# Feed-forward input matrix by seven products of quarter sums instead of eight of quarters, two of the four weight sums made by adding DMAs

## The chip, the cores and the metric

The kernel runs on one core of a Trainium2 chip. TensorE (PE) multiplies, VectorE (DVE) and ScalarE (ACT) do the elementwise work, GpSimd (POOL) does a little elementwise work, SyncE (SP) issues DMAs. The metric is device time in microseconds of one execution, the median of several runs. Smaller is better.

## The reference, cut to what matters

One layer of a streaming encoder on 544 tokens (512 of a prompt, 32 of a sample), model width 1024: attention, a recurrent branch and cross-attention are merged into `x`, and a feed-forward part of width 2816 follows. Only this last part is touched:

```
h2 = rms_norm(x, lp["norm_ffn"])                        # 544 x 1024
g_ff, u_ff = jnp.split(h2 @ lp["w_ffn_in"], 2, axis=-1) # w_ffn_in 1024 x 5632, two halves of 2816
x = x + (jax.nn.silu(g_ff) * u_ff) @ lp["w_ffn_out"]    # w_ffn_out 2816 x 1024
```

Everything is float32. To reach that accuracy at the speed of one pass, each operand is split into a high part `h` (rounded to the format fp32r) and a low part `l` (the remainder), and a product is taken as `wh*xh + wh*xl + wl*xh`: three matmuls for one.

## The kernel before

Activations lie transposed: 128 channels on the partitions, 544 tokens along the row, eight such tiles for 1024 channels (k = 0 to 7). A weight chunk is 1024 x 256, 1 MB, loaded by one DMA from SP into a `raw` buffer (there are two). It gives two weight tiles (j = 0, 1) of 128 output channels: ACT rounds 128x1024 elements into `wh` (function `A`, line 236), DVE subtracts to get `wl` (function `LO`, line 249). There are three `wh` and three `wl` buffers.

`gemm` makes one output tile of 128 channels x 544 tokens in `acc`, a pair of PSUM banks of 272 tokens each: 8 k x 3 products x 2 halves = 48 matmuls of 272 columns. All matmuls are recorded under line 308. There are two `acc` buffers.

Feed-forward: `ffn_in(i)` runs over pairs of a gate chunk and an up chunk. For each gate tile `ff_gate` multiplies by the row norm `rb` (DVE) and takes silu (ACT); for each up tile `ff_up` multiplies by `rb` and by the gate (DVE), and rounds and subtracts the result into `fh`, `flo` (tiles `ah`, `al` or `bh`, `bl`). `ffn_out(i)` multiplies by `w_ffn_out` and adds to `x2`. The 22 hidden tiles go in three parts of 8, 8 and 6: in 0, in 1, out 0, in 2, out 1, out 2. The norm factor `rb` does not exist when the first feed-forward matmul starts: the matmuls run on `x * norm_ffn` (`xgh`, `xgl`), and `rb` is applied at the evacuation. Just ahead of the feed-forward part lies the output projection `w_out`, whose evacuation (`out_evac`) makes `x2`, `xgh`, `xgl`, the squares and, after the eighth tile, `rb`.

The program's order on each engine is fixed when it is built. A planner (`Flow`) keeps a clock of estimated costs, and each piece of work is written out when its inputs are due in that plan; on the chip every engine then takes its list in order and waits for semaphores. So a late input on one engine holds up all that is listed behind it there.

Of the kernel before, what the change touches and what calls it, by code (L numbers as in the profile page):

```python
# [9 lines left out]
F32 = mybir.dt.float32  # L10
# [37 lines left out]
class Flow:  # L48
# [141 lines left out]
def hybrid_step(ctx: ExitStack, tc, io):  # L190
# [18 lines left out]
    def tl(pool, shape, dt, tag, bufs=1):  # L209
        return pool.tile(shape, dt, name=tag, tag=tag, bufs=bufs)  # L210
# [93 lines left out]
            fl.ready(out, t + 2200)  # L304
        return t + 2200

    def MM(out, lhsT, rhs, start, stop):
        nc.tensor.matmul(out, lhsT=lhsT, rhs=rhs, start=start, stop=stop)  # L308
# [41 lines left out]
    FF_PARTS = [(0, 8), (8, 8), (16, 6)]  # L350
    c_fi, c_fo = [None] * 3, [None] * 3
    for kind, i in (("in", 0), ("in", 1), ("out", 0), ("in", 2), ("out", 1), ("out", 2)):
        f0, nf = FF_PARTS[i]
        if kind == "in":
            c_fi[i] = [[chunk("w_ffn_in", 11 * s + f0 // 2 + c) for s in (0, 1)] for c in range(nf // 2)]
        else:
            c_fo[i] = [chunk("w_ffn_out", c, f0, nf) for c in range(4)]

    NQ = 2
    raws = {}  # L360
# [2 lines left out]
    def load_weights():  # L363
        for i, (src, nk) in enumerate(chunks):
            yield from fl.take("raw")
            raw = slot_tile(wpool, [P, 8, 256], F32, "raw")
            raws[i] = raw
            t = 0.0
            for j in range(2) if i == 0 else (None,):
                if j == 1:  # L370
                    yield from fl.get("mem dma")
                cs = slice(0, 256) if j is None else slice(j * P, (j + 1) * P)
                t = dma(raw[:, :nk, cs], src[:, :, cs], nk * P * (1024 if j is None else 512))
                if j is not None:
                    fl.set(("raw", i, j), t)
                    fl.set(("raw", i, j, "sent"))
            fl.set(("sent", i))
            for j in range(2):
                if ("raw", i, j) not in fl.ev:
                    fl.set(("raw", i, j), t)  # L380

    def split_weights():
        for i, (src, nk) in enumerate(chunks):
            if i in c_mem[4:]:
# [12 lines left out]
                fl.give("raw", t2)  # L397
                continue
            for j in range(2):
                yield from fl.get(("raw", i, j))  # L400
                yield from fl.take("wh", "wl")
                wh = slot_tile(wpool, [P, 8, P], F32R, "wh")[:, :nk]
                wl = slot_tile(wpool, [P, 8, P], F32R, "wl")[:, :nk]
                r = raws[i][:, :nk, j * P:(j + 1) * P]
                t = VC(wh, r) if fl.free["V"] + 1500 < fl.free["A"] else A(wh, r)
                wts[i, j] = (wh, wl)
# [4 lines left out]
            fl.give("raw", t2)  # L411

    def gemm(tiles, xh, xl, n=T, need=None):

# [3 lines left out]
        def products(acc, c, j, seq, first, last):  # L418
            wh, wl = wts[c, j]
            for q, (a, b, k) in enumerate(seq):  # L420
                w, x = (wl if a else wh), (xl if b else xh)
                for hf, m in halves:
                    s = slice(hf * m, (hf + 1) * m)
                    MM(acc[:, hf, :m], w[:, k, :], x[k][:, s] if isinstance(x, list) else x[:, k, s],
                       start=first and q == 0, stop=last and q == len(seq) - 1)
                yield None

        def finish(acc, c, j, evac):
            fl.give("wh")
# [1094 lines left out]
        return go  # L1524


    acts = [None] * 3

    def ff_gate(i, n):
        def go(acc):  # L1530
# [25 lines left out]
            fl.set(("f", i, n), t)  # L1556
        return go

    def ffn_in(i):
        f0, nf = FF_PARTS[i]  # L1560
        pool, a, b = (actp, "ah", "al") if i % 2 == 0 else (S["actb"], "bh", "bl")
        acts[i] = (tl(pool, [P, KD, T], F32R, a), tl(pool, [P, KD, T], F32R, b))
        for c in range(nf // 2):
            need = (lambda k: ("xg", k)) if i == 0 and c == 0 else None
            yield from gemm([(c_fi[i][c][0], j, ff_gate(i, 2 * c + j)) for j in range(2)], xgh, xgl, need=need)
            yield from gemm([(c_fi[i][c][1], j, ff_up(i, 2 * c + j)) for j in range(2)], xgh, xgl)

    def fo_evac(fp, i, n):
        def go(acc):
            t = VT(b2(x2[:, n]), acc[:, :, :HT], b2(x2[:, n]), OP.add)  # L1570
            give_acc(t)
            if i < 2:
                return
            yield t
            yield from square_sum(S["sq"][0], n)
        return go
# [42 lines left out]
    def ffn_out(fp, i):  # L1619
        f0, nf = FF_PARTS[i]  # L1620
        fh, flo = acts[i]
        split = 0 if i < 2 else LAST
        tiles = [(c_fo[i][n // 2], n % 2, n) for n in range(KD)]
        for n0 in range(0, KD - split, 2):
            yield from gemm([(c, j, fo_evac(fp, i, n)) for c, j, n in tiles[n0:min(n0 + 2, KD - split)]], fh, flo,
                            need=None if n0 else (lambda k: ("f", i, k)))
        if not split:
            return

        for t0, m_ in ((0, 256), (256, T - 256)):  # L1630
            for c, j, n in tiles[KD - split:]:
                yield from fl.get(("wh", c, j))
                yield from fl.take("acc")
                acc = slot_tile(accp, [P, 2, 512], F32, "acc")[:, 0, :m_]
                for q, (a, k) in enumerate([(a, k) for a in range(2) for k in range(nf)]):
                    if a == 1 and k == 0:
                        yield from fl.get(("wl", c, j))
                    for x in (fh, flo) if a == 0 else (fh,):
                        MM(acc, wts[c, j][a][:, k], x[:, k, t0:t0 + m_], q == 0 and x is fh,
                           q == 2 * nf - 1)  # L1640
                    yield None
                fl.spawn(last_evac(fp, n, (t0, m_), acc), fl.now + 60)
# [5 lines left out]
    def main():  # L1648
# [77 lines left out]
        xgh = tl(hpool, [P, KD, T], F32R, "hh")  # L1726
        xgl = tl(hpool, [P, KD, T], F32R, "hl")
# [12 lines left out]

# [4 lines left out]
def host_arrays(inputs):  # L1745
# [21 lines left out]
        a[n] = i[n].reshape(1, 64)  # L1767
    for n in ("w_in", "w_mem_kv", "w_proj_a", "w_proj_b", "w_proj_c", "w_gate", "w_out", "w_ffn_in", "w_ffn_out"):
        a[n] = tiles(i[n][0])
    rel = np.arange(REL_LO, REL_LO + REL_N)  # L1770
    n = np.abs(rel)
    large = 8 + sum((n >= t).astype(np.int64) for t in (12, 16, 23, 32, 46, 64, 91))
# [44 lines left out]
```

## Time and profile before

| | |
|---|---|
| median of 3 runs | 1230.53 us (1229.99 to 1231.04) |
| the profiled execution | 1230.78 us |
| its span, first to last instruction | 1229.0 us |
| PE busy | 1214.2 us, 99% |
| DVE busy | 678.9 us, 55% |
| ACT busy | 466.0 us, 38% |
| POOL busy | 28.2 us, 2% |
| feed-forward part | 814.2 us to the end |

The profile is of one execution. Busy time of PE is modelled, since matmuls are pipelined: the distance between the starts of two matmuls says what one costs, not its duration. On DVE and ACT too the duration of an instruction is some 0.08 us longer than the distance to the next one where two follow each other without a wait.

### The profile page before, as it was taken

How to read it: one execution, taken by the hardware profiler on the slowest of the kernel's cores; microseconds unless marked ns; L12 is line 12 of the kernel's file. 1: busy time of each engine (PE TensorE's matmuls, PEld its weight loads, DVE VectorE, ACT ScalarE, POOL GpSimd, SP SyncE). 2: the span in 40 equal slices, each digit the busy share in tenths (PEclk: the TensorE clock that was granted, in tenths of full speed). 3: DMA queues.
4: the chain of work that ended last, by engine and by line, in shares of the span. 5: the costliest groups of instructions: out<-in, count | busy, mean ns of one | idle time of the engine just before them, and what ended most of it. 6: DMA issues, size and time to landing. Idle time of an engine off the chain costs nothing.

```text
span 1229.0 us, 22475 instructions
## 1 busy us (share of the span) xinstructions
PE 1214.2 (99%) x9620; PEld 1205.5 (98%) x9620; DVE 678.9 (55%) x1340; ACT 466.0 (38%) x781; POOL 28.2 (2%) x88
## 2 busy tenths in 40 slices
PE   8999999999999999999999999999999999999996
PEld 8999999999999999999999999999999999999996
DVE  6886878787257777654455244544443443344335
ACT  6635454444335665532333232332222221222122
POOL 0002000000001001000000000000000000000001
PEclk8999999999999999999999999999999999999998
DMA  7772343321222223323422413131323222222212
GB/s 261 233 272 96 133 138 116 106 87 54 103 97 94 78 73 109 122 69 121 140 95 76 176 69 104 69 104 69 103 70 103 72 101 90 82 96 77 87 52 73
DMA packets 36835, 131.19 MB, mean 107 GB/s; under 512 B 4184, under 2 KB 15832, under 8 KB 25088
## 3 DMA queue, kind: packets, MB, share of 16 engines
q1 hardware_dynamic: 36736, 129.76, 30.9%
q8 instruction: 75, 1.23, 0.4%
q14 instruction: 24, 0.20, 0.0%
HBM read 118.81 MB, written 13.68 MB: 108 GB/s over the span
## 4 chain that ended last, share of the span: by engine, by line
PE 96%; DVE 2%; DMA 1%; ACT 0%; issue 0%; SPq 0%; DVEq 0%; ACTq 0%
PE acc L308 86%; PE side L308 8%; PE side L315 2%; DMA mk_d<-mkf 1%; DMA raw<-in_w_mem_kv 0%; DVE x L258 0%; DVE wl L249 0%; DVE xT L258 0%; DVE rst L249 0%; DVE al L249 0%; ACT wh L236 0%; DVE m L249 0%; ACT m L236 0%; SPq L300 0%; DVE hl L249 0%
## 5 line engine op out<-in xcount | busy, mean ns | idle before, releaser
L308 PE MATMUL acc<-hh,wh 128*128 128x272 f32 x1856 | 387.1, 289 | 0.0
L308 PE MATMUL acc<-hl,wh 128*128 128x272 f32 x1856 | 385.8, 289 | 0.0
L236 ACT ACTIVATE wh<-raw 128x1024 fp32r<-128x1024 f32 (+1 forms) x179 | 187.4, 1048 | 351.2 <-PE acc L308 328.3
L308 PEld LDWEIGHTS acc<-hh,wh 128*128 128x128 f32 x1856 | 290.7, 189 | 0.3
L308 PEld LDWEIGHTS acc<-hl,wh 128*128 128x128 f32 x1856 | 290.0, 188 | 0.1
L249 DVE TENSOR_TENSOR wl<-raw,wh 128x1024 fp32r<-128x1024 f32 (+1 forms) x180 | 217.1, 1207 | 95.6 <-PE acc L308 73.6
L308 PE MATMUL acc<-hh,wl 128*128 128x272 f32 x1856 | 257.2, 288 | 0.0
L308 PEld LDWEIGHTS acc<-hh,wl 128*128 128x128 f32 x1856 | 241.5, 188 | 0.1
L249 DVE TENSOR_TENSOR t<-acc,rb 128x544 f32<-128x544 f32 x44 | 31.9, 725 | 150.3 <-PE acc L308 150.0
L308 PE MATMUL acc<-ah,wh 128*128 128x272 f32 (+2 forms) x480 | 101.4, 288 | 0.0
L308 PE MATMUL acc<-al,wh 128*128 128x272 f32 (+2 forms) x480 | 101.4, 289 | 0.0
L249 DVE TENSOR_TENSOR x<-acc,x 128x544 f32<-128x544 f32 (+2 forms) x35 | 23.6, 675 | 102.7 <-PE acc L308 102.7
L308 PE MATMUL acc<-bl,wh 128*128 128x272 f32 x384 | 79.7, 289 | 0.0
L308 PE MATMUL acc<-bh,wh 128*128 128x272 f32 x384 | 79.6, 288 | 0.0
L308 PEld LDWEIGHTS acc<-ah,wh 128*128 128x128 f32 x480 | 76.4, 188 | 0.0
L308 PEld LDWEIGHTS acc<-al,wh 128*128 128x128 f32 x480 | 76.2, 188 | 0.0
L308 PE MATMUL acc<-ah,wl 128*128 128x272 f32 (+2 forms) x480 | 66.0, 288 | 0.0
L308 PEld LDWEIGHTS acc<-ah,wl 128*128 128x128 f32 x480 | 62.4, 188 | 0.0
L308 PEld LDWEIGHTS acc<-bh,wh 128*128 128x128 f32 x384 | 60.1, 189 | 0.0
L308 PEld LDWEIGHTS acc<-bl,wh 128*128 128x128 f32 x384 | 60.0, 188 | 0.0
L308 PE MATMUL acc<-bh,wl 128*128 128x272 f32 x384 | 54.0, 289 | 0.0
L308 PEld LDWEIGHTS acc<-bh,wl 128*128 128x128 f32 x384 | 50.0, 188 | 0.0
(250 smaller groups left out, 1318.1 us busy)
## 6 DMA issues: line engine op xcount, KB each, us to landing
raw<-in_w_in SPq DMA_DIRECT2D x24, 1024.0 KB, 4.9
raw<-in_w_ffn_in SPq DMA_DIRECT2D x22, 1024.0 KB, 4.9
raw<-in_w_gate SPq DMA_DIRECT2D x12, 1024.0 KB, 4.9
raw<-in_w_ffn_out SPq DMA_DIRECT2D x8, 1024.0 KB, 4.9
raw<-in_w_mem_kv SPq DMA_DIRECT2D x7, 1024.0 KB, 6.1
raw<-in_w_proj_a SPq DMA_DIRECT2D x4, 1024.0 KB, 4.9
raw<-in_w_proj_b SPq DMA_DIRECT2D x4, 1024.0 KB, 4.8
raw<-in_w_proj_c SPq DMA_DIRECT2D x4, 1024.0 KB, 4.9
```

The costliest lines, as they stand in the source:

```text
L236: nc.scalar.activation(out, in_, func, scale=scale, bias=bias, accum_out=accum_out)
L249: nc.vector.tensor_tensor(out, a, b, o)
L308: nc.tensor.matmul(out, lhsT=lhsT, rhs=rhs, start=start, stop=stop)
L315: nc.tensor.transpose(out, in_, ident[:n, :n])
```

## The change

`w_ffn_in` is handled as 22 chunks of 1024 x 256, as before. The first gate chunk and the first up chunk (`FF_PLAIN`) keep the old scheme. The other 20 are cut into four quarters A11, A12, A21, A22 (two halves of the 256 outputs, and the even and the odd k), each 128x512 elements in SBUF, and the activations into four quarters (even and odd k, two halves of 272 tokens). The output of a chunk is four blocks of 128 x 272. By the Strassen-Winograd scheme they come out of seven products, not eight; each product is 4 k x 3 matmuls of 272 columns = 12 matmuls.

- The weights need four sums. Two (`P1` = A21 + A22 and `P3` = A21 + A11) are made by DMAs that add: four plain DMAs from SP load A11 and A12, A21, a second copy of A21 (into `xb`) and A22, and two DMAs from POOL add A22 and A11 from DRAM to the two copies of A21. The other two (`P2` = P1 + A11, `P4` = P2 + A12) are DVE additions of 128x512. The signs of the scheme are carried by the activations and the evacuation (the factors -1.0).
- Seven forms are rounded by ACT and subtracted by DVE, each 128x512, into a ring of eight blocks (`hb`, `lb`: the three `wh` and `wl` buffers halved, and two blocks more in the tail of `ah`, `al`).
- The activations need four sums as well, of the normalised values, so `rb` must exist. `ff_forms` makes them in four rounds (i = 0 to 3) from the moment `rb` is there, into `bh`, `bl`, `hh`, `hl` and `m`.
- `seven` issues the products in the order A11, then A22 and P4 of the chunk before, then A12, P2, P1, P3. Sums of the output are made by letting PE accumulate on in the same bank after `quarters` has copied it out by ACT, and by DVE additions. P2 waits for the copy after A11, P3 for the copy after P2, A22 for the copy after P3, P4 for a DVE addition after that.
- The hidden tiles go in four parts of 6, 6, 6 and 4. Tiles `xgh`, `xgl` move to `ah`, `al`.

The core of the diff ("..." marks what is left out):

```diff
     def load_weights():
...
+            if i in FF_FAST:
+                yield from fl.take("xb")
+                S["xb", i] = xb = fl.pick("xb")
...
+                t = dma(b[:, :1024], d[:, :1024], 524288)
+                t = dma(b[:, 1536:], d[:, 1024:1536], 262144)
+                t = dma(xb, d[:, 1024:1536], 262144)
+                t = dma(b[:, 1024:1536], d[:, 1536:], 262144)
+                nc.gpsimd.dma_start(b[:, 1536:], d[:, 1536:], accum_op=OP.add)
+                nc.gpsimd.dma_start(xb, d[:, :512], accum_op=OP.add)
...
+    def split_ffn():
...
+            yield from split((i, "A11"), b4(q[0]))
+            if late is not None:
+                yield from late
+            yield from split((i, "A12"), b4(q[1]))
+            yield from fl.get(("raw", i, 1))
+            xb, a22, p1, p2, p3 = S["xb", i], q[2], q[3], q[0], S["xb", i]
+            VT(p2, p1, q[0], OP.add)
+            yield from split((i, "P2"), b4(p2))
+            yield from split((i, "P1"), b4(p1))
+            yield from split((i, "P3"), b4(p3))
+            late = split_late(i, b4, a22, q[1], p2, xb)
+
+    def split_late(i, b4, a22, a12, p2, xb):
+        yield from split((i, "A22"), b4(a22))
+        VT(a12, p2, a12, OP.add)
+        yield from split((i, "P4"), b4(a12))
...
+        fl.give("raw", t)
+        fl.drop("xb", xb, t)
...
+    def ff_forms():
...
+        yield from fl.get("rb")
+        for i in range(4):
+            y0, y1, u1, u2 = scratch
+            for q, y in enumerate((y0, y1)):
+                t = VX(y, x2[:, 2 * i + q], vcol("norm_ffn", 2 * i + q), S["rb"], OP.mult, OP.mult)
+            yield t
+            A(B11[0][:, i], y0[:, lo])
+            A(B2[0][:, i], y1)
+            VT(u1[:, lo], y0[:, lo], y0[:, hi], OP.subtract)
+            VX(u1[:, hi], u1[:, lo], -1.0, y1[:, hi], OP.mult, OP.subtract)
+            VT(u2[:, lo], y1[:, hi], y0[:, hi], OP.subtract)
+            t = VX(u2[:, hi], u1[:, hi], -1.0, y1[:, lo], OP.mult, OP.subtract)
+            fl.set(("xf", "B11", i), LO(B11[1][:, i], y0[:, lo], B11[0][:, i]))
+            fl.set(("xf", "B2", i), LO(B2[1][:, i], y1, B2[0][:, i]))
...
+                yield A(g[0][:, i], u)
+                t = LO(g[1][:, i], u, g[0][:, i])
...
+            for i in range(4):
+                yield from fl.get(("xf", ev, i))
+                MM(dst, wh[:, i], xh[:, i, cs], first and i == 0, False, True)
+                MM(dst, wh[:, i], xl[:, i, cs], False, False, True)
...
+            for i in range(4):
+                MM(dst, wl[:, i], xh[:, i, cs], False, last and i == 3, True)
...
+                yield from product(a, c, "A11", True, False)
+            if prev is not None:
+                yield from fl.get(("u3", prev[0]))
+                yield from product(prev[1], prev[0], "A22", False, True)
+                yield from fl.get(("c22", prev[0]))
+                yield from product(prev[2], prev[0], "P4", False, True)
...
+            yield from product(c_, c, "A12", True, True)
+            yield from fl.get(("c11", c))
+            yield from product(a, c, "P2", False, False)
...
+            yield from product(b, c, "P1", True, False)
+            yield from fl.get(("c12", c))
+            yield from product(a, c, "P3", False, False)
...
-        yield from ffn_in(0)
-        yield from ffn_in(1)
+        fl.spawn(ff_forms())
+        yield from ffn_in(0, 1)
         yield from ffn_out(fp, 0)
         yield from ffn_in(2)
         yield from ffn_out(fp, 1)
+        yield from ffn_in(3)
         yield from ffn_out(fp, 2)
+        yield from ffn_out(fp, 3)
```

Where instructions stand now is shown at three places. First DVE after `rb` exists. Before, these rows are the evacuations of the first gate and up tiles (`t1<-acc`), the gate product, and the remainders of weights (`wl`) and of the hidden tile (`al`):

```order
L249 TENSOR_TENSOR t1_9423<-acc_9303,rb_9350 128x544
L249 TENSOR_TENSOR t1_9458<-acc_9385,rb_9350 128x544
L249 TENSOR_TENSOR wl_9456<-raw_9274,wh_9455 128x1024
L249 TENSOR_TENSOR t1_9514<-acc_9452,rb_9350 128x544
L249 TENSOR_TENSOR t1_9514<-t1_9514,t1_9423 128x544
```

Now the second of the four rounds of `ff_forms` stands there among them (`fq`, `sqb` hold y0, y1, u1, u2; `bl`, `hl`, `m` receive remainders):

```order
L274 SCALAR_TENSOR_TENSOR fq_8829<-x2_8133,vec_89,rb_9344 128x544 x2
L265 TENSOR_TENSOR t1_9550<-acc_9483,rb_9344 128x544
L265 TENSOR_TENSOR fq_8829<-fq_8829 128x272
L274 SCALAR_TENSOR_TENSOR fq_8829<-fq_8829 128x272
L265 TENSOR_TENSOR sqb_8135<-fq_8829 128x272
L274 SCALAR_TENSOR_TENSOR sqb_8135<-fq_8829 128x272
L265 TENSOR_TENSOR bl_9299<-fq_8829,bh_9298 128x272
L265 TENSOR_TENSOR hl_8826<-fq_8829,hh_8825 128x544
L265 TENSOR_TENSOR wl_9303<-raw_9373,wh_9300 128x512
L265 TENSOR_TENSOR t1_9550<-t1_9550,t1_9433 128x544
```

Four such rounds were added on DVE between the evacuations of the four plain tiles and the first weight forms. Second, PE behind the fourth plain tile. Before, the fifth tile follows there on the same activations (`hh`, `hl`):

```order
L308 MATMUL acc_9508<-hh_8823,wl_9389 128x272 x16
L308 MATMUL acc_9568<-hh_8823,wh_9455 128x272 x2
L308 MATMUL acc_9568<-hl_8824,wh_9455 128x272 x2
L308 MATMUL acc_9568<-hh_8823,wh_9455 128x272 x2
L308 MATMUL acc_9568<-hl_8824,wh_9455 128x272 x2
```

Now the first product A11 follows, whose `bh`, `bl` (B11) come out of `ff_forms`, one round for each pair of rows:

```order
L325 MATMUL acc_9617<-bh_9298,wh_9245 128x272
L325 MATMUL acc_9617<-bl_9299,wh_9245 128x272
L325 MATMUL acc_9617<-bh_9298,wh_9245 128x272
L325 MATMUL acc_9617<-bl_9299,wh_9245 128x272
L325 MATMUL acc_9617<-bh_9298,wh_9245 128x272
L325 MATMUL acc_9617<-bl_9299,wh_9245 128x272
L325 MATMUL acc_9617<-bh_9298,wh_9245 128x272
L325 MATMUL acc_9617<-bl_9299,wh_9245 128x272
L325 MATMUL acc_9617<-bh_9298,wl_9302 128x272 x4
```

So the eighth row of PE here needs the fourth round of DVE. Third, DVE in the middle of the run, at the sixth of the 20 chunks. Before, weight remainders and evacuations alternate in this way:

```order
L249 TENSOR_TENSOR t1_10676<-acc_10614,rb_9350 128x544
L249 TENSOR_TENSOR t1_10676<-t1_10676,t1_10562 128x544
L249 TENSOR_TENSOR wl_10674<-raw_10476,wh_10673 128x1024
L249 TENSOR_TENSOR bl_10265<-t1_10676,bh_10264 128x544
L249 TENSOR_TENSOR t1_10736<-acc_10670,rb_9350 128x544
```

Now (`side` and `acc` are products, `raw<-raw` the additions P2 and P4, `wl` and `al` blocks of the ring, `fb` is `xb`):

```order
L265 TENSOR_TENSOR fq_8829<-side_10180,fq_8829 128x272
L265 TENSOR_TENSOR wl_9301<-raw_10081,wh_9189 128x512
L265 TENSOR_TENSOR raw_10081<-raw_10081 128x512
L265 TENSOR_TENSOR wl_9301<-raw_10081,wh_9189 128x512
L265 TENSOR_TENSOR fq_8829<-side_10180,fq_8829 128x272
L265 TENSOR_TENSOR al_8824<-raw_10081,ah_8823 128x512
L265 TENSOR_TENSOR t1_10238<-acc_10209,t1_10238 128x272
L265 TENSOR_TENSOR al_8824<-fb_8828,ah_8823 128x512
L265 TENSOR_TENSOR wl_9302<-raw_10229,wh_9245 128x512
L265 TENSOR_TENSOR wl_9302<-raw_10081,wh_9245 128x512
L265 TENSOR_TENSOR raw_10081<-raw_10081 128x512
L265 TENSOR_TENSOR wl_9303<-raw_10081,wh_9300 128x512
```

The first `raw<-raw` row waits for the adding DMA of its chunk, and evacuations that PE waits for stand behind it in the list.

## Rows read from the trace of the kernel before

**Rows 1.** The page: span, busy time of each engine with share and instructions.
```profile
span 1229.0 us, 22475 instructions
PE 1214.2 (99%) x9620; PEld 1205.5 (98%) x9620; DVE 678.9 (55%) x1340; ACT 466.0 (38%) x781; POOL 28.2 (2%) x88
```
**Rows 2.** Stretches: length, busy of PE, weight loads, DVE, ACT, POOL; clock, DMA share, GB/s.
```profile
814.22:840.60 26.38, 26.38 (x215) 26.38 (x214) 12.20 (x25) 9.29 (x11) 0.00 (x0) 1.00 0.22 70
840.60:1213.00 372.40, 372.40 (x2971) 372.40 (x2970) 148.64 (x190) 97.48 (x117) 0.00 (x0) 1.00 0.24 81
```
**Rows 3.** Timeline of PE: start, duration; first matmuls of three tiles, then 18 of 256 columns.
```profile
828.51 0.41 PE L308 MATMUL acc<-hh,wh 128*128 128x272 f32 x2
...
834.54 0.41 PE L308 MATMUL acc<-hh,wh 128*128 128x272 f32 x2
...
840.56 0.41 PE L308 MATMUL acc<-hh,wh 128*128 128x272 f32 x2
...
1200.66 0.28 PE L308 MATMUL acc<-ah,wh 128*128 128x256 f32 x1
...
1202.78 0.28 PE L308 MATMUL acc<-ah,wh 128*128 128x256 f32 x1
```
**Rows 4.** Timeline of DVE around the end of `w_out` and `rb`.
```profile
798.12 0.78 DVE L258 SCALAR_TENSOR_TENSOR hl<-x,vec,hh 128x544 fp32r<-128x544 f32 x1
798.81 0.72 DVE L249 TENSOR_TENSOR sqa<-sqa,t 128x544 f32<-128x544 f32 x1
...
825.11 0.72 DVE L249 TENSOR_TENSOR t<-acc,rb 128x544 f32<-128x544 f32 x1 [0.30 <-ACT rb L236]
...
834.74 0.72 DVE L249 TENSOR_TENSOR t<-acc,rb 128x544 f32<-128x544 f32 x1 [4.17 <-PE acc L308]
835.50 0.73 DVE L249 TENSOR_TENSOR t<-t,t 128x544 f32<-128x544 f32 x1
836.14 1.22 DVE L249 TENSOR_TENSOR wl<-raw,wh 128x1024 fp32r<-128x1024 f32 x1
837.27 0.72 DVE L249 TENSOR_TENSOR al<-t,ah 128x544 fp32r<-128x544 f32 x1
840.76 0.73 DVE L249 TENSOR_TENSOR t<-acc,rb 128x544 f32<-128x544 f32 x1 [2.77 <-PE acc L308]
```
**Rows 5.** Stretches at the start of the program, columns as in rows 2.
```profile
5.00:6.00 1.00, 0.35 (x4) 0.16 (x2) 0.64 (x2) 0.72 (x2) 0.00 (x0) 1.00 0.98 300
...
7.00:8.00 1.00, 0.09 (x1) 0.09 (x1) 0.11 (x1) 1.00 (x2) 0.00 (x0) 0.67 0.82 242
...
13.00:14.00 1.00, 1.00 (x6) 1.00 (x6) 0.15 (x1) 0.11 (x1) 0.00 (x0) 0.50 1.01 406
14.00:15.00 1.00, 1.00 (x10) 1.00 (x9) 1.00 (x2) 0.00 (x0) 0.00 (x0) 0.92 0.33 107
```
**Rows 6.** Timeline of PE there: the first matmul behind the pause.
```profile
7.91 0.58 PE L308 MATMUL acc<-memh,wh 128*128 128x256 f32 x1 [2.56 <-ACT wh L236]
```
**Rows 7.** Groups of instructions: count, busy us, mean ns of one.
```profile
L236 ACT ACTIVATE L<-acc 128x272 f32<-128x272 f32 x8 | 3.2, 399 | 4.5 <-PE acc L308 4.5
...
L236 ACT ACTIVATE gh<-graw 128x512 fp32r<-128x512 f32 x4 | 2.5, 633 | 3.9 <-DMA graw<-in_w_rg 3.9
...
L249 DVE TENSOR_TENSOR gl<-graw,gh 128x512 fp32r<-128x512 f32 x4 | 2.7, 682 | 0.3 <-ACT gh L236 0.3
...
L265 DVE CAST mh<-mraw 128x512 fp32r<-128x512 f32 x8 | 3.4, 421 | 0.0
```
**Rows 8.** DMA issues: count, size, median us from issue to landing.
```profile
raw<-in_w_ffn_in SPq DMA_DIRECT2D x22, 1024.0 KB, 4.9
...
mk_d<-mkf SPq DMA_DIRECT2D x4, 256.0 KB, 6.3
...
ck<-in_cache_mem_k SPq DMA_DIRECT2D x4, 256.0 KB, 5.4
...
o_y<-x SPq DMA_DIRECT2D x4, 256.0 KB, 2.2
```

More of the change, by code (lines that the diff above doesn't have):

```diff
@@ L63, in __init__ @@
         self.slots = {}
+        self.places = {}
     @staticmethod
@@ L169, in give, with ring, drop, pick @@
         self.slots[tag].append(self.now if at is None else at)
+    def ring(self, tag, aps, at=None):
+        for ap in aps:
+            self.drop(tag, ap, at)
+    def drop(self, tag, ap, at=None):
+        t = self.now if at is None else at
+        self.slots.setdefault(tag, []).append(t)
+        self.seq += 1
+        heapq.heappush(self.places.setdefault(tag, []), (t, self.seq, ap))
+    def pick(self, tag):
+        return heapq.heappop(self.places[tag])[2]
     def set(self, ev, at=None):
@@ L357, in hybrid_step @@
             c_fo[i] = [chunk("w_ffn_out", c, f0, nf) for c in range(4)]
+    FF_PLAIN = c_fi[0][0]
+    FF_FAST = {c for part in c_fi for pair in part for c in pair} - set(FF_PLAIN)
     NQ = 2
@@ L380, in load_weights, with split, release @@
                     fl.set(("raw", i, j), t)
+    def split(name, src):
+        yield from fl.take("hb", "lb")
+        n = src.shape[1]
+        h_, l_ = [fl.pick(g).rearrange("p (a b) -> p a b", b=P)[:, :n] for g in ("hb", "lb")]
+        t = A(h_, src)
+        blocks[name] = (h_, l_)
+        fl.set(("bh", name), t)
+        yield t
+        fl.set(("bl", name), LO(l_, src, h_))
+    def release(name):
+        for tag, ap in zip(("hb", "lb"), blocks.pop(name)):
+            fl.drop(tag, block_of(ap))
@@ L405, in split_weights @@
                 t = VC(wh, r) if fl.free["V"] + 1500 < fl.free["A"] else A(wh, r)
-                wts[i, j] = (wh, wl)
+                wts[i, j] = tuple([w[:, k] for k in range(nk)] for w in (wh, wl))
                 yield t
@@ L411, in split_weights, with free_weights @@
             fl.give("raw", t2)
+    def free_weights(c, j):
+        if (c, j) in frees:
+            for b in frees[c, j]:
+                release(b)
+        else:
+            fl.give("wh")
+            fl.give("wl")
     def gemm(tiles, xh, xl, n=T, need=None):
@@ new lines, in quarters @@
+    def quarters(c, new, a, c_, each):
+        lo, hi = slice(0, HT), slice(HT, T)
+        yield from fl.get(("done", c, "A11"))
+        t0 = yield from new()
+        t = A(t0[:, lo], a)
+        fl.set(("c11", c), t)
+        yield from fl.get(("done", c, "A12"))
+        t = VT(t0[:, lo], c_, t0[:, lo], OP.add)
+        yield t
+        each(t0, 0, lo, t0[:, lo])
+        yield from fl.get(("done", c, "P2"))
+        t = A(t0[:, hi], a)
+        fl.set(("c12", c), t)
+        yield from fl.get(("done", c, "P1"), ("done", c, "P3"))
+        b = S["b", c]
+        t1 = yield from new()
+        t = A(t1[:, hi], a)
+        fl.set(("u3", c), t)
+        yield t
+        t = VT(t1[:, hi], b, t1[:, hi], OP.add)
+        fl.set(("c22", c), t)
+        yield t
+        each(t1, 1, hi, t1[:, hi])
+        yield from fl.get(("done", c, "A22"))
+        each(t1, 1, lo, a)
+        give_acc(fl.when(t1[:, lo]))
+        yield from fl.get(("done", c, "P4"))
+        t = VT(t0[:, hi], b, t0[:, hi], OP.add)
+        fl.give("side", t)
+        yield t
+        each(t0, 0, hi, t0[:, hi])
+        return t0, t1
@@ new lines, in fast_gate, with new, go, each @@
+    def fast_gate(i, n):
+        def new():
+            yield from fl.take("ft")
+            return fl.pick("ft")
+        def go(c, a, c_):
+            def each(g, j, cs, src):
+                A(g[:, cs], src, AF.Silu, scale=-1.0 if j else 1.0)
+            g = yield from quarters(c, new, a, c_, each)
+            S["fg", i, n] = g
+            fl.set(("fg", i, n), fl.when(g[0]))
+        return go
+    def fast_up(i, n):
+        def new():
+            yield from fl.take("t1")
+            return t1_tile()
+        def go(c, a, c_):
+            def each(u, j, cs, src):
+                if j:
+                    VX(u[:, cs], src, -1.0, S["fg", i, n][1][:, cs], OP.mult, OP.mult)
+            u = yield from quarters(c, new, a, c_, each)
+            g = S["fg", i, n]
+            t = VT(u[0], u[0], g[0], OP.mult)
+            for q in g:
+                fl.drop("ft", q, t)
+            fh, flo = acts[i]
+            for j in (1, 0):
+                yield A(fh[:, n + j], u[j])
+                t = LO(flo[:, n + j], u[j], fh[:, n + j])
+                fl.give("t1", t)
+                fl.set(("f", i, n + j), t)
+        return go
@@ L1557, in ff_up, with ffn_plain, ffn_in @@
         return go
[L1559 to L1566, printed above, removed]
+    def ffn_plain():
+        need = lambda k: ("xg", k)
+        g, u = FF_PLAIN
+        yield from gemm([(g, j, ff_gate(0, j)) for j in range(2)], xgh, xgl, need=need)
+        yield from gemm([(u, j, ff_up(0, j)) for j in range(2)], xgh, xgl)
+    def ffn_in(*parts):
+        run = []
+        for i in parts:
+            x = ("bh", "bl") if i % 2 == 0 else ("ah", "al")
+            for q in range(len(c_fi[i])):
+                if (i, q) != (0, 0):
+                    run += [(c_fi[i][q][0], fast_gate(i, 2 * q)), (c_fi[i][q][1], fast_up(i, 2 * q))]
+            acts[i] = [S[n][:, :6 * T].rearrange("p (k t) -> p k t", k=6) for n in x]
+        if 0 in parts:
+            yield from ffn_plain()
+            for tag, nme in (("hb", "ah"), ("lb", "al")):
+                add_blocks(tag, [S[nme][:, 6 * T:6 * T + 512], S[nme][:, 6 * T + 512:6 * T + 1024]])
+        yield from seven(run)
     def fo_evac(fp, i, n):
```

141 lines of the change are left out of this document (127 added, 14 removed).

## The prediction

> **What bounds the kernel now.** I read the page's busy times first: PE 99%, DVE 55%, ACT 38%, POOL 2% [rows 1]. Then the stretches of the feed-forward part: PE is busy without a break, at full clock, from 814.2 to 1213.0 us, while DVE is busy 149 of 372 us (40%) and ACT 97 (26%) [rows 2]. So the time there is the number of matmuls times what one costs, and only what changes that number, or makes PE wait, moves the end. What one costs is read from starts: tiles of 48 matmuls begin at 828.51, 834.54 and 840.56 [rows 3], 6.03 us apart, 0.1256 us for one of 272 columns. In the old scheme neighbours alternate between two banks; in the new one twelve in a row add into one bank. The 18 matmuls of 256 columns in one bank at 1200.66 to 1202.78 take 0.118 each [rows 3], in step with their columns, so I charge the new ones 0.1256 too.
>
> **What goes away.** Twenty chunks need 84 matmuls instead of 96: 240 matmuls, 20 x 12 x 0.1256 = **-30.1 us**. A product takes 1.51 us, a chunk 10.55 instead of 12.06. `w_ffn_out` keeps its 1056 matmuls; eight more additions to `x2` there hide behind PE (DVE was at 40%). Parts of 6, 6, 6 and 4 move work about, and the last part is shorter by a third, but the chain behind its last matmul is the same: 0, give or take 1.
>
> **The start of the new scheme.** The first product needs all four rounds of `ff_forms`, and these need `rb`. The rows by which to cost this are on DVE. `rb` is there at 825.1 [rows 4] (the norm's own order hardly changes). The fourth plain tile, with which PE has something to do without the forms, ends at 840.6, where the fifth tile begins [rows 3]. DVE prices are distances between neighbours: a scaled row of 544 costs 0.69 (798.12 to 798.81), one of 1024 costs 1.13 (836.14 to 837.27), one of 544 costs 0.65 (835.50 to 836.14, rounded up), and if the next one reads what it wrote, 0.76 (834.74 to 835.50) [rows 4]. Along the line through 544 and 1024, 512 elements cost 0.62 and 272 cost 0.38. A round is then two scaled rows (1.38), four half rows, two of them dependent (1.8), and remainders of 272 and three times 544 (0.38 + 1.95): 5.5 us. Up to the B11 remainder of the fourth round that is 3 x 5.5 + 3.55 = 20.05. Between them stand in DVE's order four evacuations of plain tiles (2.6), two gate products (1.5), two remainders of hidden tiles (1.3), eight weight remainders (5.0) and two weight additions (1.3): 11.7 us. The sum is 31.75, so from 825.3 the fourth B11 remainder is done at 857.0. Nothing that these rows wait for is later: the last plain tile's evacuation comes 18.2 us into that list (843.5, where PE is done at 840.8), and the first adding DMA, started when a `raw` buffer comes free at about 819, has 13 us.
>
> PE meanwhile has 6 matmuls of the first product (0.75 us) and idles otherwise: 857.0 - 840.6 - 0.75 = **+15.6 us**. It idles in two pieces, about 8 and 7 us. At the start of the program PE had stopped in the slice that begins at 5 us, its granted clock was half by 7.3 (0.67 over that slice), it resumed at 7.91 and got the full clock back at 14.1 [rows 5, 6]. Here too it will come back to 1.2 GHz and run some 6.2 us on it, at half the pace: **+3.0 us** (from 0, if the clock holds, to 3.5).
>
> **The end of each run of products.** Where a run ends (three times), nothing stands between the last P3 and A22 of the same chunk, which waits for ACT to copy 272 columns: 0.40 us [rows 7], plus the 0.2 from the end of a tile to its evacuation (840.56 to 840.76) [rows 3, 4] and as much back: 3 x 0.77 = **+2.3 us**.
>
> **The middle.** Per gate chunk DVE has nine rows of 512 (5.6) and three of 272 (1.1), per up chunk 5.6 + 1.1 and two products of 272, a product of 544 and two remainders (2.9): 16.3 us per pair against 21.1 of PE, 77%. ACT has seven roundings (0.63 each less 0.08 in a row [rows 7]) and 5 to 7 short rows: some 12.5 us per pair. Neither is a bound on average. But the order is fixed and the waits are close: P3 waits for a copy of 0.4 us that may start when P2 ends and must be done 1.51 us later, with one rounding of 0.55 ahead of it on ACT; A22 likewise behind P3. That leaves 0.3 to 0.9 us. I cannot read from the trace how often it is missed, since nothing there is so tight: PE waited for ACT for 0 us in this part. Ends: 0 and 0.6 us per chunk (one rounding too many in front each time). I take 0.18, nearer to 0 as the plan leaves some room: **+3.5 us** (0 to 12).
>
> **The adding DMAs.** The trace has none, and no DMA from POOL. What hides them: a buffer comes free with the P4 remainder of chunk c, and chunk c+2's forms wait for DVE's addition that needs the sum. In DVE's order seven products lie between the two, 10.5 us, and DVE and ACT can be some 3 us late there before a copy that PE waits for is held up: the cover is about **13.5 us**. The need: the plain loads are 1.25 MB instead of 1 MB, which took 4.9 us [rows 8], so 6.1; then one adding DMA of 256 KB, which waits for all loads of its buffer. DMAs of 256 KB took 2.2 (an output) to 6.3 us (to DRAM), a load among others 5.4 [rows 8]. Sum 8.3 to 12.4, taken 11.5. Inside the cover, so **0**; from 13.5 on each microsecond more costs one per pair of chunks, some nine pairs. The Trainium skill, "DMA: Bandwidth & Descriptors", section "Anatomy of one DMA", gives 2.0 us plus bytes/436 GB/s for a DMA from GpSimd, estimated 2.6 us here; the sum would be 8.7 by it, and the term 0 as well.
>
> **Sum.** -30.1 + 15.6 + 3.0 + 2.3 + 3.5 = -5.7 us. The profiled execution took 1230.78 (its span 1229.0 and 1.8 around it), 0.25 above the median of 1230.53. 1230.78 - 5.7 = 1225.1; I say **1225**.
>
> **Rivals.**
> 1. *The adding DMAs come late* (the slower side). DVE's addition then holds evacuations behind it, and PE waits. At a need of 15 us it costs 1.5 x 9 = 13.5 us: **1238**; it passes the old time at 14.2. For it: DVE works nearly twice as densely as before, and POOL has to prepare DMAs beside it. Against it: 2 us of room over the dearest end. The Trainium skill, "SBUF — State Buffer", section "SBUF: two separate sides", says that a DMA from GpSimd cannot write its descriptors while DVE runs a two-port copy within SBUF. The trace's one fast form of 512, the cast, takes 421 ns against 682 for a subtraction [rows 7], and the feed-forward part has only subtractions, products and additions on DVE, so by that rule nothing is held. Chance 0.13.
> 2. *The fixed order rubs*: 0.6 us per chunk, 12 instead of 3.5: **1233.5**. For it: 77% on DVE with waits in both directions; against it: a margin of 0.3 to 0.9 us at each of the waits. Chance 0.17.
> 3. *The start is cheaper*: if DVE had only the forms themselves before the fourth round's B11 (20 us), PE would idle 4 us, keep most of its clock, and the end were **1212**. Against it: the other 11.7 us stand ahead of it in DVE's list. Chance 0.12.
> 4. *The forecast*, 1219 to 1229: 0.58.
>
> **Range and chances.** The range takes the forecast with its bounds (start 13 to 18, clock 0 to 3.5, middle 0 to 12), the third rival's nearer half and the second: 1215 to 1236. A measurement of this kernel tells 0.2% (2.5 us) from no change. Faster, below 1228: nine tenths of the forecast and the third rival, 0.64. Same, to 1233: the rest of the forecast and half of the second rival, 0.15. Slower: 0.21.
>
> **What would show it.** Right: a gap of PE of 14 to 18 us shortly after 840, ended by DVE's `bl` of the fourth round, then about 6 us at half clock; after that matmuls 0.1256 apart and products of 1.51 us; three gaps of 0.8 us that end with an ACT copy; 2928 matmuls of 272 or like columns in the feed-forward part instead of 3168; DVE at 75 to 80% between the `ffn_out` stages. Wrong: PE waits that end with a DMA of POOL's queue or with DVE's `raw<-raw`; PE waits in every chunk for ACT's copies; matmuls of a product further apart than 0.126; or no gap at 841.

## The result, and the profile after

The changed kernel takes 1246.44 us (median, 1245.97 to 1249.51) against 1230.78 before in the same comparison: ratio 1.0133, 95% interval 1.0116 to 1.0151. It is **slower by 15.7 us**; 1225 was forecast. The page of the changed kernel, with the lines that answer to [rows 1], and PE's busy share and granted clock in 40 slices:

```profile
span 1243.9 us, 22824 instructions
PE 1197.2 (96%) x9380; PEld 1180.2 (95%) x9380; DVE 772.8 (62%) x1594; ACT 537.0 (43%) x1013; POOL 63.5 (5%) x128
PE   8999999999999999999999999995999999998996
PEclk8999999999999999999999999997999999999998
```

PE has 240 matmuls fewer, as meant, but the span is 14.9 us longer. The hole in the 28th slice was forecast. The rest of the loss is too fine for the slices; PE's waits from 812 us on show it (the eight largest sums; who waited <- for whom: us in sum, times, longest):

```profile
PE acc L325 <- ACT bh L252: 9.7, 2, 6.0
PE acc L325 <- DVE fq L265: 6.5, 10, 1.0
PE acc L325 <- DVE t L265: 5.4, 10, 0.6
PE side L325 <- DVE rsy L274: 3.1, 2, 2.8
PE acc L325 <- ACT fq L252: 2.9, 4, 1.3
PE acc L325 <- DVE bl L265: 2.4, 2, 2.2
PE side L325 <- DVE sqa L265: 2.0, 2, 1.1
PE acc L325 <- ACT t L252: 1.5, 3, 0.5
```

Lines 1 and 6 are the hole. Lines 2 and 3 are ten and ten: one wait in each of the 20 chunks, always in P2, of which the forecast knew nothing. PE and DVE around one of them:

```profile
884.69 0.29 PE L325 MATMUL acc<-hl,wh 128*128 128x272 f32 x1
885.51 0.40 PE L325 MATMUL acc<-hh,wh 128*128 128x272 f32 x1 [0.53 <-DVE fq L265]
...
885.02 0.44 DVE L265 TENSOR_TENSOR fq<-acc,fq 128x272 f32<-128x272 f32 x1 [0.67 <-PE acc L325]
```

The two matmuls are the second and the third of P2. The third starts 0.82 us behind the second instead of 0.1256: 0.69 lost. It waits for DVE, which at 885.02 adds A12's result out of PSUM. A12 and P2 write into different banks and need nothing of each other. But both banks are halves of one `acc` tile, and the program, as written, orders a write to a tile behind every read of that tile that stands earlier. In the written order of PE's work the wait can be read at every P2, here the first three matmuls of one (`DVE_49` is the semaphore that DVE counts up):

```
L325 MATMUL acc<-hh,ah 128x272
L325 MATMUL acc<-hl,ah 128x272
L325 MATMUL acc<-hh,ah 128x272 [waits DVE_49]
```

The third and not the first is held because the planner wrote DVE's addition down just behind the second. So it is in 15 of the chunks; in five the addition stands ahead of P2, and the first matmul waits.

By stretches, from starts on PE, against the 0.1256 us per matmul of [rows 3]: the plain tiles end at 843.34 instead of 840.56 (+2.8); the first run of ten chunks takes 132.0 instead of 105.5 (+26.5); the second of six 70.95 instead of 63.3 (+7.65); the third of four 48.3 instead of 42.2 (+6.1); the last part, less its matmuls, 16.6 instead of 14.8 (+1.8). Sum +44.8, less 30.1 for the matmuls removed: +14.7, against 14.9 of the spans.

### The profile page after: what moved, and what is told of

Its sections match the earlier page's. It is cut to its first block, busy times and chain, and to the rows that moved or that the text cites. A ratio compares the mean times of both kernels' runs of the same rounds, so it can differ in the third digit from the quotient of the medians.

```text
span 1243.9 us, 22824 instructions
## 1 busy us (share of the span) xinstructions
PE 1197.2 (96%) x9380; PEld 1180.2 (95%) x9380; DVE 772.8 (62%) x1594; ACT 537.0 (43%) x1013; POOL 63.5 (5%) x128
## 4 chain that ended last, share of the span: by engine, by line
PE 91%; DVE 6%; ACT 1%; issue 1%; DMA 1%; SPq 0%; DVEq 0%; ACTq 0%
PE acc L325 76%; PE side L325 13%; PE side L332 2%; DVE wl L265 1%; DMA raw<-in_w_mem_kv 1%; DVE t L265 1%; ACT wh L252 0%; DVE al L265 0%; DVE fq L265 0%; DVE x L274 0%; DVE hl L265 0%; DVE raw L265 0%; DVE fq L274 0%; DVE rst L265 0%; DVE bl L265 0%
## 5 line engine op out<-in xcount | busy, mean ns | idle before, releaser
L252 ACT ACTIVATE wh<-raw 128x1024 fp32r<-128x1024 f32 (+2 forms) x251 | 199.2, 801 | 259.7 <-PE acc L325 194.8
L265 DVE TENSOR_TENSOR wl<-raw,wh 128x512 fp32r<-128x512 f32 (+1 forms) x252 | 225.6, 905 | 125.7 <-PE acc L325 75.9
L325 PE MATMUL acc<-hh,wh 128*128 128x272 f32 x1268 | 274.0, 292 | 10.5 <-DVE fq L265 5.4
L325 PE MATMUL acc<-hl,wh 128*128 128x272 f32 x1268 | 270.8, 290 | 0.0
L325 PEld LDWEIGHTS acc<-hh,wh 128*128 128x128 f32 x1268 | 203.0, 189 | 14.3 <-DVE fq L265 6.3
L325 PEld LDWEIGHTS acc<-hl,wh 128*128 128x128 f32 x1268 | 202.6, 188 | 0.1
L325 PE MATMUL acc<-hh,wl 128*128 128x272 f32 x1268 | 180.9, 289 | 0.0
L325 PEld LDWEIGHTS acc<-hh,wl 128*128 128x128 f32 x1268 | 166.9, 188 | 0.1
L325 PE MATMUL acc<-bh,wh 128*128 128x272 f32 x464 | 100.3, 289 | 9.7 <-ACT bh L252 9.7
L325 PE MATMUL acc<-bl,wh 128*128 128x272 f32 x464 | 100.2, 290 | 2.4 <-DVE bl L265 2.4
L325 PEld LDWEIGHTS acc<-bh,wh 128*128 128x128 f32 x464 | 74.9, 189 | 10.2 <-ACT bh L252 10.2
```

Of the source, the lines that this page charges most:

```text
L252: nc.scalar.activation(out, in_, func, scale=scale, bias=bias, accum_out=accum_out)
L265: nc.vector.tensor_tensor(out, a, b, o)
```

## The experiments

**1. A bank tile of its own for A12.**

```diff
-                a, c_ = acc[:, 0, :HT], acc[:, 1, :HT]
+                a = acc[:, 0, :HT]
...
+            yield from fl.take("side")
+            c_ = side_tile()[:, :HT]
```

> The product A12 gets a PSUM bank of its own (a tile of the pool side) instead of the second bank of the same acc tile; nothing else is changed. Theory: in the changed kernel the third matmul of every P2 waits for the DVE addition that reads A12 only because both banks are one tile, so that a write to one bank is held until the other has been read. The gaps there add up to 15.1 us over 20 chunks, and two more of 1.45 us at the first A12 of the second and third run have the same cause: 18 us. Expected 1246.4 - 18, plus 0 to 3 us for waits that are hidden behind these gaps today: 1228 to 1232, and no row of PE any more that waits for DVE fq or DVE t in the middle of P2. Rival: DVE is late as such and the wait moves to the next product that needs DVE or ACT: 1240 to 1246, with gaps of 0.5 us and more in most chunks, at P3, A22 or P4.

Measured: 1229.16 us, ratio to before 0.9991 (0.9982 to 1.0), 17.3 us less than the changed kernel and inside the theory's range. The theory holds. A12, P2 and DVE's addition at one place of this kernel:

```profile
880.37 0.67 PE L325 MATMUL side<-hh,al 128*128 128x272 f32 x4
880.88 0.29 PE L325 MATMUL acc<-hh,wh 128*128 128x272 f32 x1
881.00 0.28 PE L325 MATMUL acc<-hl,wh 128*128 128x272 f32 x1
881.13 0.29 PE L325 MATMUL acc<-hh,wh 128*128 128x272 f32 x1
...
881.08 0.44 DVE L265 TENSOR_TENSOR fq<-side,fq 128x272 f32<-128x272 f32 x1 [0.41 <-PE side L325]
```

The first line is A12 (its bank is now in `side`), the others are P2. The addition runs beside P2's matmuls and holds none. In the whole feed-forward part no matmul of a product waits for DVE `fq` or `t` any more. The largest two of PE's waits there (columns as above):

```profile
PE acc L325 <- ACT bh L252: 9.7, 2, 6.0
PE acc L325 <- ACT fq L252: 3.2, 5, 0.9
```

**2. The same tile, DVE's addition written later.**

```diff
-        yield from fl.get(("done", c, "A12"))
-        t = VT(t0[:, lo], c_, t0[:, lo], OP.add)
-        yield t
-        each(t0, 0, lo, t0[:, lo])
         yield from fl.get(("done", c, "P2"))
         t = A(t0[:, hi], a)
         fl.set(("c12", c), t)
+        t = VT(t0[:, lo], c_, t0[:, lo], OP.add)
+        yield t
+        each(t0, 0, lo, t0[:, lo])
```

> A12 stays in the second bank of the acc tile as in the changed kernel; only the DVE addition that reads A12's result is written later in the program, behind P2 and ACT's copy of it, instead of behind the second matmul of P2. It separates the order in which the program is written from where the banks lie. Theory: PE is held because the addition on the same tile stands ahead of P2's third matmul in the program; written behind P2 it holds nothing that is near. The 15.1 us at P2 go, the two waits of 1.45 us at the first A12 of a run stay, P3 (the next product into this tile) may wait up to 0.2 us: 1246.4 - 15.1 = 1231.3, between 1230 and 1235. Rival (two banks of one tile must be far apart in time for another reason, or DVE's list is then late at P3): 1238 to 1247.

Measured: 1229.47 us, ratio 1.0003 (0.999 to 1.0016), just under the theory's range. Three lines moved, no bank and no instruction changed, and 17 us are gone. So it is neither the place of the banks nor DVE's load: it is where the read stands in the written order. The read still holds what stands behind it: P3, the next product into the tile, waits for DVE at three places, by up to 0.74 us where 0.2 was expected, 1.9 us in sum. The two waits of 1.29 (1.44 lost) at the first A12 of the second and third run are still there, as expected; there the read that stands ahead is ACT's copy of A11's bank, behind a late rounding. PE's waits for ACT's copies and for DVE's additions in this trace:

```profile
PE acc L325 <- ACT fq L252: 3.1, 3, 1.3
...
PE acc L325 <- DVE fq L265: 1.5, 2, 0.7
PE acc L325 <- DVE t L265: 0.4, 1, 0.4
```

**3. A second plain pair, alone and with the own bank.**

```diff
-    FF_PLAIN = c_fi[0][0]
+    FF_PLAIN = c_fi[0][0] + c_fi[0][1]
```

> The second pair of chunks too keeps the old scheme, so that PE has 24 us more to do that needs no activation sums; 18 chunks instead of 20 are done by seven products. Theory: PE's stall at the start (14.3 us lost between 843.7 and 859.2) is DVE's list of sums and weight forms behind the late norm, and work that does not need them covers it. It costs 24 matmuls, 3.0 us; the stall shrinks to under 3 us, and two of the gaps at P2 (1.2 and 0.7 us) go: 1246.4 + 3.0 - 12 - 1.9 = 1235.5, between 1233 and 1238. Rival: DVE's list grows with the plain tiles as PE's does, and the stall moves instead of shrinking: 1243 to 1250.

> Own bank for A12 and two plain pairs together. Theory: both causes are separate and their gains add: from 1230 by the bank alone, less 9 for the start, 1221, between 1218 and 1225, which is under the kernel before by 6 to 12 us. Rival (waits only move): not under 1231.

Measured: 1231.51 us alone (ratio 1.0008, 0.9999 to 1.0017), 1216.04 with the own bank (0.9886, 0.987 to 0.9903). Both lie below the ranges of their theories. Alone it gains 14.9 us, more than the 11 expected, since the hole went as a whole and not down to 3 us, and the half clock behind it with it; with the bank 30.4, where the two single gains (17.3 and 14.9) add to 32.2 and share two waits at P2. The stretches of the hole, first of the changed kernel, then of the second plain pair alone (columns as in [rows 2]):

```profile
842.00:850.00 8.00, 1.99 (x17) 1.78 (x16) 7.96 (x14) 3.22 (x7) 0.00 (x0) 0.82 0.00 1
850.00:858.00 8.00, 1.88 (x4) 0.96 (x4) 7.96 (x17) 3.99 (x7) 0.00 (x0) 0.50 0.51 157
```

```profile
842.00:850.00 8.00, 8.00 (x66) 8.00 (x65) 7.96 (x16) 4.94 (x9) 1.94 (x2) 1.00 0.57 170
850.00:858.00 8.00, 8.00 (x66) 8.00 (x65) 7.96 (x15) 4.44 (x8) 0.00 (x0) 1.00 0.88 221
```

DVE is busy without a break in both: it is what the hole waits for. The same list, from the first form to the fourth `bl`, takes about as long when PE has other work: 30.8 us in the changed kernel, 32.0 here with one operation more.

**4. The weight sums by DVE instead of adding DMAs.**

```diff
-                nc.gpsimd.dma_start(b[:, 1536:], d[:, 1536:], accum_op=OP.add)
-                nc.gpsimd.dma_start(xb, d[:, :512], accum_op=OP.add)
...
+            VT(p1, p1, a22, OP.add)
+            VT(p3, p3, q[0], OP.add)
             VT(p2, p1, q[0], OP.add)
```

> The two weight sums that the adding DMAs make are made by two DVE additions of 128x512 per chunk, and nothing is left on POOL's queue; the four plain loads stay. Theory: the adding DMAs are never what PE waits for (no wait of PE or DVE of the changed kernel ends with one), so taking them away gains nothing; DVE has 40 additions of 0.6 us, 24 us, more to do, most of it in time that DVE has free: 1246.4, between 1245 and 1250. Rival: the adding DMAs are late and hold DVE's sums: faster by 2 to 10 us, 1236 to 1244.

Measured: 1264.72 us, 18.3 slower than the changed kernel, outside both ranges. Both theories fall: without the adding DMAs nothing is gained, and the 24 us that they take from DVE were not idle time either. One place, PE, ACT and DVE:

```profile
891.40 0.77 PE L325 MATMUL acc<-m,wh 128*128 128x272 f32 x4 [1.49 <-ACT fq L252]
...
890.11 0.63 ACT L252 ACTIVATE ah<-raw 128x512 fp32r<-128x512 f32 x1 [2.98 <-DVE raw L265]
890.65 0.41 ACT L252 ACTIVATE fq<-fq 128x272 f32<-128x272 f32 x1
890.97 0.38 ACT L252 ACTIVATE fq<-acc 128x272 f32<-128x272 f32 x1
...
887.98 0.69 DVE L265 TENSOR_TENSOR raw<-raw 128x512 f32<-128x512 f32 x1
888.59 0.68 DVE L265 TENSOR_TENSOR fb<-fb,raw 128x512 f32<-128x512 f32 x1
889.30 0.69 DVE L265 TENSOR_TENSOR raw<-raw 128x512 f32<-128x512 f32 x1
```

P3 waits for the copy at 890.97. P2 had ended at about 888.3 and ACT was idle, but ahead of it in ACT's list stands the rounding of P2's weights, and that waits for the third of three additions on DVE. DVE is at 75% over 880 to 960 (59.9 of 80 us), and still operations put ahead of a chain cost most of their length, 18.3 of the 24 us.

**5. The cover of the adding DMAs.** The edit repeats the adding DMA of P1.

> The changed kernel with the adding DMA of P1 issued twice, one after the other into the same 256 KB (so P1 is A21 + 2 A22: the weights are not those of the reference). It prices the cover of the adding DMAs. In the trace of the changed kernel the loads of a buffer start at 886.72, its adding DMA at 892.62, landing takes 4.3 us, so the sum is there at about 896.9, and DVE takes it at 900.14: a need of 10.2 us, a cover of 13.4. A second addition that must wait for the first adds one landing, about 4.3 to 5 us: a need of 14.5 to 15.2, 1.1 to 1.8 us over the cover. Theory (the cover is the time between two places in DVE's list): DVE's sums now wait for a DMA, and a chunk takes up to 1.8 us longer: 1256 to 1282. Rival (weight forms are made so far ahead that a late sum is absorbed): 1246 to 1249.

Measured: 1275.69 us, 29 slower than the changed kernel, in the theory's range. DVE's sum now waits for the DMA (11 times, 36.1 us between 860 and 1240), ACT's rounding waits for the sum, the copies behind it wait, and PE with them. Two issues, a sum and a wait of PE:

```profile
895.26 0.86 POOL L402 DMA_DIRECT2D raw<-in_w_ffn_in  x1 [10.12 <-DMA raw<-in_w_ffn_in]
899.73 0.86 POOL L402 DMA_DIRECT2D raw<-in_w_ffn_in  x1 [3.60 <-DMA raw<-in_w_ffn_in]
...
904.35 0.69 DVE L265 TENSOR_TENSOR raw<-raw 128x512 f32<-128x512 f32 x1 [2.89 <-DMA raw<-in_w_ffn_in]
...
906.10 1.15 PE L325 MATMUL acc<-m,wh 128*128 128x272 f32 x7 [2.04 <-ACT t L252]
```

**6. Order of the products and size of the parts**, on the kernel with own bank and two plain pairs. The first edit puts P4 of the chunk before between P2 and P1 and, in a run's last chunk, P3 ahead of P1; the second is `FF_PARTS = [(0, 6), (6, 6), (12, 4), (16, 6)]`.

> Own bank and two plain pairs as before, and the order of the products is A11, A22 of the chunk before, A12, P2, P4 of the chunk before, P1, P3, so that two products instead of one stand between P2 and P3; in the last chunk of a run P3 comes before P1, so that P1 stands between P3 and A22. Theory: what is left of the waits are copies of 272 columns by ACT that stand behind a rounding and have one product of 1.5 us, or at a run's end nothing, to be done in: P3 0.36 to 1.08 us seven times, 4.7 us in sum, run ends 1.9 us. Two products cover copy and rounding: 1216.0 - 1.9 - 3.5 (the first chunk of a run still has one product between) = 1210.6, between 1209 and 1213. Rival: P4 and c22, or the weight forms that are now used in another order than they are made, become late instead: 1214 to 1220.

> As the kernel with two products between, and the hidden tiles go in parts of 6, 6, 4 and 6 instead of 6, 6, 6 and 4. Theory: with only four hidden tiles in the last part the chain of the final norm has less matmul work beside it; the last part of the changed kernel took 40.7 us, of which 24.1 are its 192 matmuls, 16.6 the rest; before 50.9 - 36.2 = 14.7. With six tiles the rest is 14.7 again: 1.9 us less than with 6, 6, 6, 4: 1208.7, between 1207.5 and 1211. Rival: the rest of 16.6 has another cause and stays: no change.

> Own bank, two plain pairs and parts of 6, 6, 4, 6, in the order of products of the changed kernel. It separates the parts from the order: the kernel with two products between and these parts took 1212.8, the one without either 1216.0, the one with the order alone 1215.8. Theory: the order is worth nothing and the parts 3 us: 1213, between 1212 and 1214. Rival: the two only gain together: 1215 to 1216.5.

Measured: order alone 1215.84, both 1212.79 (ratio 0.9855, 0.9839 to 0.9872), parts alone 1215.58. The order alone, and the parts alone, came out in the ranges of their rivals, both together above the theory's range. The order alone brought nothing: the waits at run ends went (3 x 0.65), and two waits of 1.0 us for ACT `wh` (A12's weight form, now used one place earlier) and smaller ones of this kind came. The parts should have given 1.9: with the order they gave 3.0, alone 0.5 by the medians; by the spans 2.3 and 1.1 (1213.3 to 1211.0, 1213.8 to 1212.7). Single executions of these kernels lie up to 3 us apart, so the medians alone do not settle it. The traces do: the last part, less its matmuls, falls from 16.0 to 14.6 us with the order and from 16.0 to 14.6 without it. The parts give 1.4 by themselves; that the two only gain together is not shown. What the parts do can be seen at the end, PE's wait for the last squares, changed kernel and the one with both edits:

```profile
1230.50 0.72 PE L325 MATMUL side<-ones_d,sqa 128*128 128x1 f32 x5 [1.05 <-DVE sqa L265]
```

```profile
1198.14 0.83 PE L325 MATMUL side<-ones_d,sqa 128*128 128x1 f32 x6 [0.26 <-DVE sqa L265]
```

In the kernel before the same wait was 0.27. The version with both edits beats the kernel before by 17.7 us.

**7. The changed kernel once more.**

> The changed kernel once more, unchanged, for a second trace of its start. In its first trace PE waits 0.9 us for the last sum of squares at 818 us, and 16 matmuls from 821.12 on take 2.97 us instead of 2.01, at a granted clock of 0.72 over 818 to 824. In the traces of the variants with an own bank (and of the one with DVE sums) the wait is there and the clock stays at 1.00. If the fall of the clock belongs to the changed kernel, it is there again; if it comes by chance after such a wait, it is there in some traces and not in others. Time 1246.4 either way, within 2 us.

Measured: 1247.65 us. The clock fell, but elsewhere: not at 818 to 824, where it now stayed at 1.00, but for longer behind the hole (last section). So the fall at 818 comes in some traces and not in others. The four plain tiles with the norm among them took 27.6 us here and 29.1 in the first trace; before it was 26.3.

## Why the prediction was wrong, point by point

- **Removed matmuls, -30.1: right.** In the kernel with the own bank, where chunks run undisturbed, products A11 start 10.51 apart, against 10.55 forecast:

```profile
864.34 0.29 PE L325 MATMUL acc<-bh,wh 128*128 128x272 f32 x1
...
874.85 0.29 PE L325 MATMUL acc<-bh,wh 128*128 128x272 f32 x1
```

- **The start, +15.6: the end of the hole right within 1 us, in part by luck; 13.7 lost.** The fourth `bl` was to be done at 857.0; PE goes on at 857.90, behind the DVE row of 857.41. DVE's list held exactly the operations that were counted, but began at 827.04 instead of 825.3, behind the late norm, and took 30.8 us instead of 31.75; the two errors cancel in part:

```profile
843.70 0.29 PE L325 MATMUL acc<-bl,wh 128*128 128x272 f32 x1
850.00 0.60 PE L325 MATMUL acc<-bh,wh 128*128 128x272 f32 x1 [6.01 <-ACT bh L252]
...
855.14 0.59 PE L325 MATMUL acc<-bh,wh 128*128 128x272 f32 x1 [3.71 <-ACT bh L252]
857.90 0.59 PE L325 MATMUL acc<-bl,wh 128*128 128x272 f32 x1 [2.16 <-DVE bl L265]
...
857.41 0.43 DVE L265 TENSOR_TENSOR bl<-fq,bh 128x272 fp32r<-128x272 f32 x1
```

- **The norm ahead of it, "the order hardly changes", 0: wrong by 2.8.** It moves PE's stop from 840.6 to 843.3, so the hole itself is shorter. DVE's last addition to the squares now stands behind one more weight remainder of 512, and PE waits 0.93 us for it (0 before) in all eleven traces of this kernel and its variants. That, with the first matmuls behind it, is 1.2 of the 2.8. The other 1.6 are the clock, which fell after that wait in this trace.
- **Half clock, +3.0:** about 1.5 in the first trace, about 3.7 in the second (last section). Right in kind.
- **Run ends, +2.3: right.** Three waits of 0.49 for ACT `t`, 0.64 lost at each: 1.9.
- **The middle, +3.5 (0 to 12): the step that failed.** The three runs exceed their matmuls by 40.2 us; less the hole (13.7), the half clock (1.5) and the run ends (1.9) that is 23.1, 1.15 per chunk instead of 0.18. Of it 15.1 are P2's waits, 2.9 those at the first A12 of a run, 2.1 four others, and the rest is the first matmul after each wait, which takes 0.1 longer than its successors. I took the list of waits from the scheme, which result needs which: P2 needs the copy after A11, P3 the copy after P2. That list has no wait of P2 for DVE's addition. Nor had the signs of being wrong: they named waits in every chunk, but for ACT's copies. The wait comes from the tile that holds both banks, and it stood in the order as written, which I had and read for what stands where, not for which matmul waits for whom. The rival "the fixed order rubs" (0.6 per chunk, 1233.5) had the place but neither the cause nor the size: the rubbing that I meant, copies behind roundings on ACT, is the 3.2 us of `ACT fq` in experiment 1.
- **Adding DMAs, 0: right in the first trace.** Cover forecast 13.5, measured 13.4 at one chunk (loads issued at 886.72, the sum that needs them at 900.14); need forecast 11.5, measured 10.2: 5.9 of loads, then 4.3 of landing. That the covers agree is partly luck: the forecast was 10.5 us of DVE's list and 3 of slack behind it, the 13.4 are the list alone. Timeline rows of the changed kernel (SP's queue, POOL, DVE):

```profile
886.72 1.28 SPq L316 DMA_DIRECT2D raw<-in_w_ffn_in  x2
...
892.62 0.86 POOL L401 DMA_DIRECT2D raw<-in_w_ffn_in  x1 [13.14 <-DMA raw<-in_w_ffn_in]
...
900.14 0.69 DVE L265 TENSOR_TENSOR raw<-raw 128x512 f32<-128x512 f32 x1
```

  and of its DMA issues, which [rows 8] lacked (count, size, median us to landing):

```profile
raw<-in_w_ffn_in POOLq DMA_DIRECT2D x20, 256.0 KB, 4.3
fb<-in_w_ffn_in POOLq DMA_DIRECT2D x20, 256.0 KB, 5.5
```

  At the start the margin was smaller. In the second trace of the changed kernel DVE's first sum waited 1.25 us for its adding DMA: the buffer's loads began at 818.36, this adding DMA alone took 7.9 us to land, and DVE went on at 833.32, a need of 14.9 us, over the forecast's dearest end. PE does not wait for this sum, but for the list that it stands in, and the hole lost 14.3 instead of 13.7. Of the other traces only that of experiment 5 has a wait of DVE for an adding DMA. The row of the second trace:

```profile
833.32 0.69 DVE L265 TENSOR_TENSOR raw<-raw 128x512 f32<-128x512 f32 x1 [1.25 <-DMA raw<-in_w_ffn_in]
```

  Experiment 5 shows that the rival stood 3 us away, and its price was too low: one more landing, 1 to 2 us over the cover by the rows of the changed kernel, cost 29 us, not 1 to 2 for each of nine pairs. There the plain loads of 256 KB took 6.8 instead of 4.9, so the need grew by more than the landing, and DVE waited up to 5.8 us at once.
- **The tail, 0 give or take 1: +1.8.** Two hidden tiles fewer in the last part leave less matmul work beside the final norm; experiment 6 gets 1.4 back with a last part of six.

Of the 20.4 us between the forecast sum (-5.7) and the measured one (+14.7) the middle has 19.6; the norm and the tail (4.6 over) and the hole, the half clock and the run ends (3.8 under) nearly cancel. Without the failing step (1246.4 - 17) the changed kernel takes 1229.2 to 1229.5, no measurable difference to before and still 4 over the forecast. In the trace of experiment 1 the middle still has some 8 us instead of 3.5, in waits for copies on ACT and for weight forms; the norm and the tail are 3.0 over, the other terms 3.7 under.

## What to carry to other kernels

Two PSUM banks in one tile are one thing to the program: a product into one bank waits for every read of the other that is written ahead of it (20 of 20 here). Before costing a pipeline of this kind, read for each matmul which engine it waits for in the order as written, and price every wait at the distance matmul end to next matmul (0.7 us here) unless a product stands between. And a share of 60 to 75% on an engine with a fixed list is not room: operations put ahead of a chain that PE waits for cost most of their length (18.3 of 24 us in experiment 4), and one moved behind the chain's next step costs little (experiment 2). Experiment 4 was not repeated without the wait at P2, so what the additions cost there is not shown.

## What was not expected of the hardware

- Behind the hole PE's clock fell to 0.50 of full speed, that is 1.2 GHz, in all six traces that have the hole, but how long it stayed there after PE resumed differs for the same kernel. Two traces of the changed kernel from the end of the hole on (columns as in [rows 2]), the earlier one first:

```profile
860.00:862.00 2.00, 1.59 (x10) 1.37 (x8) 1.43 (x3) 0.82 (x2) 0.00 (x0) 0.80 0.83 139
862.00:864.00 2.00, 1.38 (x11) 1.38 (x12) 1.04 (x2) 0.60 (x3) 0.00 (x0) 1.00 0.70 112
```

```profile
860.00:862.00 2.00, 0.98 (x5) 0.66 (x4) 0.89 (x2) 1.21 (x3) 0.00 (x0) 0.50 0.87 130
862.00:864.00 2.00, 2.00 (x10) 2.00 (x10) 0.15 (x1) 0.19 (x2) 0.00 (x0) 0.50 0.03 4
864.00:866.00 2.00, 2.00 (x12) 2.00 (x11) 0.69 (x1) 0.85 (x2) 0.00 (x0) 0.55 0.00 0
```

  In both, PE waits 1.03 and 1.02 us for the first P2; in the first trace that wait came after the clock had risen (862.62), in the second before (861.61). Whether it held the clock down there is not shown.

  A wait of only 0.93 us at about 818 was followed by 0.72 over 818 to 824 in three traces (the changed kernel's first, the second plain pair's, the doubled DMA's) and by 1.00 in the other eight. Why, no run here shows.
- Adding DMAs of 256 KB landed in 4.3 us (P1) and 5.5 (P3), and plain loads of the same size beside them in 4.9. The Trainium skill, "DMA: Bandwidth & Descriptors", section "Anatomy of one DMA", gives 2.0 us plus bytes/436 GB/s for a DMA from GpSimd, an estimated 2.6 us for this size; the trace does not agree. POOL was busy 0.86 to 1.2 us with each issue while DVE was two thirds busy (53.4 of 80 us from 880 on).
